# Merging the 32-block inverses of a gated DeltaNet with 128-row, half-width tiles padded by zeros

## The chip, the cores and the metric

The kernel runs on one core of one Trainium2 chip. The metric is the device time of one execution in microseconds (us). The five engines of the core are TensorE (PE in the profile, with its weight loads as PEld), VectorE (DVE), ScalarE (ACT), GpSimd (POOL) and SyncE (SP, which here issues the DMAs).

## The reference

One inference step of a two-layer decoder trunk for 512 prompt tokens and 8 x 8 sample tokens, with a width of 1024, all in float32. Layer 0 mixes by causal pooling, layer 1 by a gated DeltaNet; each mixer is followed by a SwiGLU block (inner width 2816), and all have RMS norms before and after. What the change touches is the triangular solve in the chunked delta rule:

```python
a_mat = jnp.where(strict, jnp.einsum('bhnid,bhnjd->bhnij', kb, k) * decay, 0.0)
t_mat = a_mat + jnp.eye(CHUNK, dtype=jnp.float32)
solve = functools.partial(lax.linalg.triangular_solve, left_side=True, lower=True, unit_diagonal=True)
u = solve(t_mat, v * beta[..., None])
w = solve(t_mat, kb * jnp.exp(gc)[..., None])
...
def step(S, inp):
    v_new = u_i - jnp.einsum('bhck,bhkv->bhcv', w_i, S)
    o_i = jnp.einsum('bhck,bhkv->bhcv', qd_i, S) + jnp.einsum('bhcs,bhsv->bhcv', qk_i, v_new)
    S = S * gl_i[..., None, None] + jnp.einsum('bhck,bhcv->bhkv', kd_i, v_new)
```

There are 16 value heads of 128 x 128. The kernel works in chunks of 128 tokens, four for the prompt.

## The kernel before, in words

The whole program is recorded first and then ordered by a planner (class Plan). Each operation is put with its engine or engines, an estimated cost and the operations that it must follow; a list scheduler with 40 rounds of search then writes an order for all engines. Two accesses to one PSUM tile, one of which writes, always keep the order in which they were recorded; accesses to SBUF tiles keep it only where their regions meet. Where the planner expects PE to stand free it puts in fillers, matmuls of ones on ones into a free PSUM bank (ps_w in the profile). Its costs know the height and the width of a matmul's tile.

The DeltaNet runs in four groups of four value heads. For a group, project computes queries, keys and values with matmuls (ps_m) and a short convolution on DVE. Then core does this:

- It forms Uw, a tile of 128 partitions x 16 matrices x 128 columns: for each of 4 heads and 4 chunks the transposed triangular matrix of the solve.
- inv32 inverts the four 32 x 32 blocks on the diagonal of each of the 16 matrices at once on DVE (tiles "ia" and "ii"), and ends with four DVE transposes, one for each row block of 32 partitions, from "ii" into the diagonal blocks of Uw. Beside it runs the preparation of the sample tokens (sample_front).
- The merge turns the inverses of 32-blocks into those of 64-blocks and then of 128. T01 holds diagonal blocks transposed back by DVE. For two lower blocks each: a product of an off-diagonal block of Uw with a block of T01 goes to PSUM and by ACT to Rs; a second product with a diagonal block goes by ACT, negated, into the off-diagonal block of Uw. The same is then done once more with 64-blocks, through R2. The matmuls use tiles of the array of 32 x 32 and then of 64 x 64, in places given by tile_position (row, column).
- scan goes through the four chunks with the merged Uw and carries the state S from chunk to chunk; sample_heads does the sample tokens with states loaded by DMA into the tiles tagged "ia" and "ii", and with km in the tile tagged "T01".

The matmuls of the next group's project (in the last group, of the output projection out0) are free to run beside all this. Uw is one tile for all groups, so the forming of Uw for the next group waits for the scan of this one.

Tiles of one tag share memory; with bufs=1 the next tile of the tag waits for the last reader of the one before. PSUM is handed out in rings of banks by bank(tag): "s" has three banks, "k" two.

In the profile all recorded operations have line 281, the line at which the planner issues them, so tiles are told apart by name; digits at the end of a name are dropped: T is T01, R is R2, Rs is Rs. An fp32 matmul leaves two records of a MATMUL and two of a LDWEIGHTS.

Of the kernel before, what the change touches and what calls it, by code (L numbers as in the profile page):

```python
# [11 lines left out]
F32 = mybir.dt.float32  # L12
F32R = mybir.dt.float32r
I32 = mybir.dt.int32
AF = mybir.ActivationFunctionType
# [5 lines left out]
P = 128  # L21
# [474 lines left out]
def hybrid_kernel(  # L496
# [11 lines left out]
    PE, ACT, DVE, POOL, SP = (plan.engine(**{name: real}) for name, real in (  # L508
        ("PE", nc.tensor), ("ACT", nc.scalar), ("DVE", nc.vector), ("POOL", nc.gpsimd), ("SP", nc.sync)))
# [76 lines left out]
    def bank(tag, shape=(P, 512)):  # L586
        i = RING[tag][turns[tag] % len(RING[tag])]
        turns[tag] += 1
        idle = psp.tile([P, 512], F32, name="ps_w", tag="b%d" % i, bufs=1)
        t = psp.tile(list(shape), F32, name="ps_" + tag, tag="b%d" % i, bufs=1)  # L590
        plan.bank(i, idle, t)
        return t
# [243 lines left out]
    with ExitStack() as s0:  # L836
        xp = pool("xp0", stack=s0)
        x = xp.tile([P, NC, T], F32, name="x")
        y = {o0: xp.tile([P, NC, n], F32, name="y%d" % o0) for o0, n in HALVES}
        tp = pool("tp0", stack=s0)  # L840
        with ExitStack() as st:
# [12 lines left out]
            for g0, src in ((G_MPRE, norm_mix_pre), (G_MPOST, norm_mix_post), (G_FPRE, norm_ffn_pre),  # L854
                            (G_FPOST, norm_ffn_post), (G_PS, pool_scale)):
                n = src.shape[0] * NC
# [72 lines left out]
            for hi, (o0, n) in enumerate(HALVES):  # L929
                tag = "AB"[hi]  # L930
# [77 lines left out]
    def inv32(ap_, W):  # L1008


        A = ap_.tile([P, 32, 32], F32, name="ia", tag="ia", bufs=1)
        XT = ap_.tile([P, 2, 512], F32, name="ii", tag="ii", bufs=1)
        X = XT[:, 0].rearrange("p (j i) -> p j i", j=32)
        for b in range(4):
            s = slice(32 * b, 32 * b + 32)
            DVE.transpose(A[s], W[s, :, 32 * b:32 * b + 32].rearrange("p h i -> p i h").unsqueeze(2)
                          .to_broadcast([32, 32, 2, 16]))
            yield 1.2
        EITHER.tensor_copy(X, eye2)
        for m in range(31, 0, -1):  # L1020
            lo = m // 2
            tv = XT[:, 1, :m * (16 - lo)].rearrange("p (j i) -> p j i", j=m)
            DVE.tensor_tensor(tv, A[:, m, :m].unsqueeze(2).to_broadcast([P, m, 16 - lo]),
                              X[:, m:m + 1, lo:].to_broadcast([P, m, 16 - lo]), op=mult)
            DVE.tensor_tensor(X[:, :m, lo:], X[:, :m, lo:], tv, op=sub)
            yield 2 * (m * (16 - lo) + 60) / 700
        for b in range(4):
            s = slice(32 * b, 32 * b + 32)
            DVE.transpose(W[s, :, 32 * b:32 * b + 32].rearrange("p h (i d) -> p i d h", d=2),
                          X[s].rearrange("p j i -> p i j"))  # L1030
            yield 0.6


    with ExitStack() as st:
# [214 lines left out]
        def braid(a, b, n):  # L1249

            for i, c in enumerate(a):
                yield c
                if i % n == n - 1:
                    c = next(b, None)
                    if c is not None:
                        yield c
            yield from b
# [208 lines left out]
        def core(G, pr_, out):  # L1466
            qk, vt, qks, vs, kt = pr_
            QD = cp_.tile([P, 4, SPANS, P], F32, name="QD", tag="QD", bufs=1)
            oss = cp_.tile([P, SP1, 4], F32, name="oss", tag="oss", bufs=2)
            POOL.memset(oss[:, SPANS], 1.0)  # L1470
            out.append(oss)
            TQ = cp_.tile([P, 2, 2, P], F32, name="TQ", tag="TQ", bufs=1)
            Ts, Qs = TQ[:SMP], TQ[SMP:, :, :, :SMP]
            ks = cp_.tile([P, 2, P], F32R, name="ks", tag="ks", bufs=1)
            Uv = Uw.rearrange("p (h s) i -> p h s i", h=4)
            h4 = slice(4 * G, 4 * G + 4)
            for s in range(SPANS):
                ps = bank("s", (P, 4, P))
                gts = cp_.tile([P, 2, 4, P], F32R, name="gts", tag=("T01", "ia")[s % 2], bufs=1)
                for i, src in enumerate((gH, gL)):  # L1480
                    gt = gts[:, i]
                    EITHER.tensor_tensor(gt, t_le.unsqueeze(1).to_broadcast([P, 4, P]),
                                      src[:, s, h4].bitcast(F32).unsqueeze(2).to_broadcast([P, 4, P]), op=mult)
                    PE.matmul(ps, t_gt_r, gt, start=i == 0, stop=i == 1)
                de = QD[:, :, s]
                ACT.activation(de, ps, AF.Exp)
                EITHER.tensor_tensor(de, de, t_le.unsqueeze(1).to_broadcast([P, 4, P]), op=mult)
            for s in range(SPANS):
                sl = slice(s * P, (s + 1) * P)
                de = QD[:, :, s]  # L1490
                for hd in range(2):
                    pk = bank("k")
                    pkv = pk[:, :2 * P].rearrange("p (x i) -> p x i", x=2)
                    PE.matmul(pkv, qk[:, hd, 0, sl], qk[:, hd, :, sl], start=True, stop=True)
                    for e in range(2):
                        h = 2 * hd + e
                        DVE.scalar_tensor_tensor(out=Uv[:, h, s], in0=pkv[:, 0],
                                                 scalar=bet[:, s, 4 * G + h:4 * G + h + 1], in1=de[:, h],
                                                 op0=mult, op1=mult)
                    DVE.tensor_tensor(QD[:, 2 * hd:2 * hd + 2, s], pkv[:, 1:2].to_broadcast([P, 2, P]),  # L1500
                                      de[:, 2 * hd:2 * hd + 2], op=mult)
                    yield 0.6
            yield from braid(inv32(cp_, Uw), sample_front(G, qks, Ts, Qs, ks), 8)
            T01 = cp_.tile([P, 16, 64], F32, name="T01", tag="T01", bufs=1)
            POOL.memset(T01[:32, :, 32:], 0.0)
            for b, o in ((0, 0), (1, 32), (2, 0)):
                q = slice(32 * b, 32 * b + 32)
                DVE.transpose(T01[q, :, o:o + 32], Uw[q, :, 32 * b:32 * b + 32])
                yield 0.6

            Rs = cp_.tile([P, 16, 32], F32, name="Rs", tag="Rs", bufs=1)
            Q = [slice(32 * b, 32 * b + 32) for b in range(4)]
            prs = [bank("k", (P, 16, 32)) for _ in range(2)]
            for u in range(16):
                for i, b0 in enumerate((0, 2)):
                    PE.matmul(prs[i][Q[b0 + 1], u], Uw[Q[b0], u, Q[b0 + 1]], T01[Q[b0], u, 0:32], start=True, stop=True,
                              tile_position=(32 * b0, 32 * b0 + 32))
            for i, b0 in enumerate((0, 2)):
                ACT.activation(Rs[Q[b0 + 1]], prs[i][Q[b0 + 1]], AF.Copy)
            pus = [bank("s", (P, 16, 32)) for _ in range(3)]  # L1520
            for u in range(16):
                for i, (q, c) in enumerate(((1, 0), (3, 2), (1, 1))):
                    l, r = (Uw[Q[q], u, Q[q]], Rs[Q[q], u]) if i == 2 else (Rs[Q[q], u], Uw[Q[q], u, Q[q]])
                    PE.matmul(pus[i][Q[c], u], l, r, start=True, stop=True, tile_position=(32 * q, 32 * c))
            for i, b0 in enumerate((0, 2)):
                ACT.activation(Uw[Q[b0], :, Q[b0 + 1]], pus[i][Q[b0]], AF.Copy, scale=-1.0)
            ACT.activation(T01[Q[1], :, 0:32], pus[2][Q[1]], AF.Copy, scale=-1.0)

            R2 = cp_.tile([P, 16, 64], F32, name="R2", tag="ia", bufs=1)
            E = [slice(0, 64), slice(64, P)]  # L1530
            prs = [bank("k", (P, 8, 64)) for _ in range(2)]
            for u in range(8):
                for i in range(2):
                    PE.matmul(prs[i][E[i], u], Uw[:64, 8 * i + u, 64:], T01[:64, 8 * i + u], start=True, stop=True,
                              tile_position=(0, 64 * i))
            for i in range(2):
                ACT.activation(R2[64:, 8 * i:8 * i + 8], prs[i][E[i]], AF.Copy)
            pus = [bank("s", (P, 8, 64)) for _ in range(2)]
            for u in range(8):
                for i in range(2):  # L1540
                    PE.matmul(pus[i][E[i], u], R2[64:, 8 * i + u], Uw[64:, 8 * i + u, 64:], start=True, stop=True,
                              tile_position=(64, 64 * i))
            for i in range(2):
                ACT.activation(Uw[:64, 8 * i:8 * i + 8, 64:], pus[i][E[i]], AF.Copy, scale=-1.0)
            yield from braid(scan(G, qk, vt, QD, kt, Uv, oss), sample_heads(G, qks, vs, Ts, Qs, ks, oss), 2)

        def gate_norm(pr_, oss):
# [238 lines left out]
```

## Time and profile before

| what | value |
|---|---|
| median of 3 runs | 1669.38 us (1666.42 to 1671.91) |
| profiled execution, time | 1672.26 us |
| profiled execution, span | 1670.6 us |
| mean granted clock of TensorE | 0.977 |
| PE busy | 1640.1 us, 98% |
| DVE busy | 1005.8 us, 60% |
| ACT busy | 696.3 us, 42% |
| POOL busy | 94.3 us, 6% |

The profile is of one execution; its times are in us from the start of its span. Busy time is the union of an engine's records; a matmul's record reaches beyond the start of the next one, since they are pipelined, so the distance between starts tells what one costs. The granted clock is the share of the full TensorE clock that the chip allowed.

### The profile page before, as it was taken

To read this page: it belongs to the slowest core of one execution; us is meant where nothing else is said; L and a number is where in the kernel's file an instruction comes from. 1 tells how busy PE (TensorE), PEld (TensorE's weight loads), DVE (VectorE), ACT (ScalarE), POOL (GpSimd) and SP (SyncE) were. 2 spreads that over 40 slices of the span, in tenths; PEclk is the share of its full clock that TensorE was granted. 3 is DMA by queue.
4 is the path that set the end of the run, shared out by engine and by line. 5 is a ranking of instruction groups with operands and counts; after the bars stand their busy time and mean duration, and the time that the engine had idled before them with its cause. 6 is when DMAs were issued, how large, how long until landed. Compare 5 with 4: busy or idle time off the path is not lost.

```text
span 1670.6 us, 30880 instructions
## 1 busy us (share of the span) xinstructions
PE 1640.1 (98%) x12495; PEld 1584.6 (95%) x12495; DVE 1005.8 (60%) x2096; ACT 696.3 (42%) x1423; POOL 94.3 (6%) x231
## 2 busy tenths in 40 slices
PE   9999999999999899999999999999999999999998
PEld 8999999999999789998999899899999999999997
DVE  6874223332597996797899689767596222223345
ACT  7653222222466534463453355324364223222244
POOL 4000000000010200010120011000000000000000
PEclk9999999999999998998999899899999999999999
DMA  6354322232356114334333422554755223323333
GB/s 173 103 154 124 92 86 78 75 102 75 114 166 164 51 52 134 87 97 119 97 97 94 135 70 78 159 168 145 237 146 150 85 77 90 93 70 89 89 109 112
DMA packets 329814, 185.27 MB, mean 111 GB/s; under 512 B 12236, under 2 KB 324141, under 8 KB 329408
## 3 DMA queue, kind: packets, MB, share of 16 engines
q1 hardware_dynamic: 329671, 183.30, 37.9%
q8 instruction: 98, 1.61, 0.4%
q14 instruction: 45, 0.36, 0.1%
HBM read 157.73 MB, written 25.77 MB: 110 GB/s over the span
## 4 chain that ended last, share of the span: by engine, by line
PE 86%; DVE 7%; ACT 3%; issue 2%; POOL 1%; DMA 1%; DVEq 0%; ACTq 0%; SPq 0%; POOLq 0%
PE ps_B L281 30%; PE ps_A L281 23%; PE ps_m L281 17%; PE ps_s L281 6%; PE ps_k L281 5%; PE ps_x L281 2%; DVE ii L281 2%; PE ps_e L281 1%; DVE wl L281 1%; PE ps_n L281 1%; ACT L281 1%; ACT wh L281 1%; PE ps_g L281 1%; DMA yo<-y_d 1%; DVE Uw L281 0%
## 5 line engine op out<-in xcount | busy, mean ns | idle before, releaser
L281 ACT ACTIVATE wh<-wraw 128x1024 fp32r<-128x1024 f32 (+1 forms) x259 | 267.7, 1036 | 493.3 <-PE ps_A L281 161.6
L281 DVE TENSOR_TENSOR wl<-wraw,wh 128x1024 fp32r<-128x1024 f32 (+1 forms) x252 | 304.7, 1213 | 275.1 <-PE ps_A L281 104.8
L281 PE MATMUL ps_m<-hH,wh 128*128 128x320 f32 (+1 forms) x832 | 245.9, 319 | 1.0 <-ACT u L281 0.6
L281 PE MATMUL ps_m<-hH,wl 128*128 128x320 f32 (+1 forms) x832 | 242.0, 314 | 4.7 <-DVE wl L281 4.7
L281 PE MATMUL ps_m<-hL,wh 128*128 128x320 f32 (+1 forms) x832 | 242.4, 314 | 1.2 <-DVE hL L281 1.2
L281 PE MATMUL ps_B<-hH,wl 128*128 128x320 f32 x768 | 219.3, 311 | 0.0
L281 PE MATMUL ps_B<-hH,wh 128*128 128x320 f32 x768 | 219.1, 311 | 0.0
L281 PE MATMUL ps_B<-hL,wh 128*128 128x320 f32 x768 | 218.0, 311 | 0.0
L281 PE MATMUL ps_A<-hH,wh 128*128 128x256 f32 x768 | 206.6, 283 | 2.2 <-DVE yo L281 1.8
L281 PE MATMUL ps_A<-hL,wh 128*128 128x256 f32 x768 | 206.2, 283 | 0.0
L281 PE MATMUL ps_A<-hH,wl 128*128 128x256 f32 x768 | 203.6, 283 | 0.0
L281 PEld LDWEIGHTS ps_m<-hH,wl 128*128 128x128 f32 x832 | 153.9, 192 | 9.0 <-DVE wl L281 4.9
L281 PEld LDWEIGHTS ps_m<-hH,wh 128*128 128x128 f32 x832 | 153.7, 193 | 7.5 <-ACT u L281 1.9
L281 PEld LDWEIGHTS ps_m<-hL,wh 128*128 128x128 f32 x832 | 154.2, 192 | 5.3 <-DVE hL L281 2.1
L281 PEld LDWEIGHTS ps_A<-hH,wh 128*128 128x128 f32 x768 | 141.9, 190 | 2.9 <-issue 2.5
L281 PEld LDWEIGHTS ps_A<-hL,wh 128*128 128x128 f32 x768 | 142.2, 190 | 0.2
L281 PEld LDWEIGHTS ps_A<-hH,wl 128*128 128x128 f32 x768 | 141.4, 190 | 0.1
L281 PEld LDWEIGHTS ps_B<-hH,wl 128*128 128x128 f32 x768 | 139.5, 189 | 0.6 <-DVE wl L281 0.5
L281 PEld LDWEIGHTS ps_B<-hH,wh 128*128 128x128 f32 x768 | 139.5, 189 | 0.2
L281 PEld LDWEIGHTS ps_B<-hL,wh 128*128 128x128 f32 x768 | 139.2, 189 | 0.1
L281 PE MATMUL ps_B<-aH,wl 128*128 128x320 f32 x352 | 102.8, 311 | 0.0
L281 PE MATMUL ps_B<-aH,wh 128*128 128x320 f32 x352 | 102.5, 311 | 0.0
(386 smaller groups left out, 3119.5 us busy)
## 6 DMA issues: line engine op xcount, KB each, us to landing
wraw<-in_ffn_w_in_dram SPq DMA_DIRECT2D x112, 512.0 KB
wraw<-in_gdn_w_in_dram SPq DMA_DIRECT2D x56, 512.0 KB
wraw<-in_ffn_w_out_dram SPq DMA_DIRECT2D x48, 448.0 KB
wraw<-in_gdn_w_out_dram SPq DMA_DIRECT2D x24, 512.0 KB
wraw<-in_ffn_w_out_dram SPq DMA_DIRECT2D x16, 512.0 KB
St<-in_state_gdn_rec_dram SPq DMA_DIRECT2D x32, 256.0 KB
out_dram<-St SPq DMA_DIRECT2D x32, 256.0 KB
z_d<-zz SPq DMA_DIRECT2D x16, 288.0 KB
```

What stands on the lines that cost most here:

```text
L281: calls[e](*a, **k)
```

## The change

The steps of the merge keep their products, but each matmul now takes 128 rows of the array and 64 of its columns, with operands padded by zeros, two matmuls for the left and the right half of the columns in turn. T01, Rs2 (in the slot "ii") and the lower half of R2 (in "ia") are set to zero by POOL first. T01 holds the transposed block 0 in its first 32 columns and block 2 in the others for the first step; after it, block 1 is transposed into the second columns and block 2 set back to zero. The second step is two series, pt with 32 and pu with 64 streamed columns, and its results leave PSUM in six copies of 256 columns instead of three of 512. Rs, formerly a tile of its own that shared a tag with a scratch tile, is dropped for Rs2.

```diff
+            T01 = cp_.tile([P, 16, 64], F32, name="T01", tag="T01", bufs=1)
+            Rs = cp_.tile([P, 16, 64], F32, name="Rs2", tag="ii", bufs=1)
+            R2 = cp_.tile([P, 16, 64], F32, name="R2", tag="ia", bufs=1)
+            for t in (T01, Rs, R2[:64]):
+                POOL.memset(t, 0.0)
+            def odd(un):
+                return Uw[:, un].rearrange("p (x b) -> p x b", x=2)[:, :, 32:]
+            def products(pr, l, r, n=64):
+                for u in range(8):
+                    for i in range(2):
+                        PE.matmul(pr[E[i], u, :n], l(8 * i + u), r(8 * i + u), start=True, stop=True,
+                                  tile_position=(0, 64 * i))
+            def out_of(pr, to, j, c, scale=1.0):
+                for i in range(2):
+                    q = 64 * i + 32 * j
+                    ACT.activation(to(slice(8 * i, 8 * i + 8)), pr[q:q + 32, :, c], AF.Copy, scale=scale)
-            for b, o in ((0, 0), (1, 32), (2, 0)):
-                q = slice(32 * b, 32 * b + 32)
-                DVE.transpose(T01[q, :, o:o + 32], Uw[q, :, 32 * b:32 * b + 32])
+            lo, up = slice(0, 32), slice(32, 64)
+            for b, c in ((0, lo), (2, up)):
+                DVE.transpose(T01[Q[b], :, c], Uw[Q[b], :, Q[b]])
-            prs = [bank("k", (P, 16, 32)) for _ in range(2)]
+            pr = bank("k", (P, 16, 32))
             for u in range(16):
-                for i, b0 in enumerate((0, 2)):
-                    PE.matmul(prs[i][Q[b0 + 1], u], Uw[Q[b0], u, Q[b0 + 1]], T01[Q[b0], u, 0:32], start=True, stop=True,
-                              tile_position=(32 * b0, 32 * b0 + 32))
+                for i, c in enumerate((lo, up)):
+                    PE.matmul(pr[E[i], u], Uw[:, u, E[i]], T01[:, u, c], start=True, stop=True, tile_position=(0, 64 * i))
...
+            ACT.activation(Rs[Q[1], :, lo], pr[Q[1]], AF.Copy)
+            ACT.activation(Rs[Q[3], :, up], pr[Q[3]], AF.Copy)
+            DVE.transpose(T01[Q[1], :, up], Uw[Q[1], :, Q[1]])
+            POOL.memset(T01[Q[2], :, up], 0.0)
-            pus = [bank("s", (P, 16, 32)) for _ in range(3)]
-            for u in range(16):
-                for i, (q, c) in enumerate(((1, 0), (3, 2), (1, 1))):
-                    l, r = (Uw[Q[q], u, Q[q]], Rs[Q[q], u]) if i == 2 else (Rs[Q[q], u], Uw[Q[q], u, Q[q]])
-                    PE.matmul(pus[i][Q[c], u], l, r, start=True, stop=True, tile_position=(32 * q, 32 * c))
+            pu, pt = bank("s", (P, 8, 64)), bank("s", (P, 8, 64))
+            products(pt, lambda un: Uw[:, un, :64], lambda un: Rs[:, un, lo], 32)
+            products(pu, lambda un: Rs[:, un], odd)
+            out_of(pt, lambda us: T01[Q[1], us, lo], 1, lo, -1.0)
+            out_of(pu, lambda us: Uw[Q[0], us, Q[1]], 0, lo, -1.0)
+            out_of(pu, lambda us: Uw[Q[2], us, Q[3]], 1, up, -1.0)
...
+            pr = bank("k", (P, 8, 64))
+            products(pr, lambda un: Uw[:, un, 64:], lambda un: T01[:, un])
             for i in range(2):
-                ACT.activation(R2[64:, 8 * i:8 * i + 8], prs[i][E[i]], AF.Copy)
+                ACT.activation(R2[64:, 8 * i:8 * i + 8], pr[E[i]], AF.Copy)
+            pu = bank("s", (P, 8, 64))
+            products(pu, lambda un: R2[:, un], lambda un: Uw[:, un, 64:])
             for i in range(2):
-                ACT.activation(Uw[:64, 8 * i:8 * i + 8, 64:], pus[i][E[i]], AF.Copy, scale=-1.0)
+                ACT.activation(Uw[:64, 8 * i:8 * i + 8, 64:], pu[E[i]], AF.Copy, scale=-1.0)
```

More of the change, by code (lines that the diff above doesn't have):

```diff
@@ L1503, in core @@
             yield from braid(inv32(cp_, Uw), sample_front(G, qks, Ts, Qs, ks), 8)
+            Q = [slice(32 * b, 32 * b + 32) for b in range(4)]
+            E = [slice(0, 64), slice(64, P)]
             T01 = cp_.tile([P, 16, 64], F32, name="T01", tag="T01", bufs=1)
-            POOL.memset(T01[:32, :, 32:], 0.0)
-            for b, o in ((0, 0), (1, 32), (2, 0)):
-                q = slice(32 * b, 32 * b + 32)
-                DVE.transpose(T01[q, :, o:o + 32], Uw[q, :, 32 * b:32 * b + 32])
+            Rs = cp_.tile([P, 16, 64], F32, name="Rs2", tag="ii", bufs=1)
@@ L1509, in core @@
+            def out_of(pr, to, j, c, scale=1.0):
[5 more added lines that the diff above has]
+                DVE.transpose(T01[Q[b], :, c], Uw[Q[b], :, Q[b]])
                 yield 0.6
-            Rs = cp_.tile([P, 16, 32], F32, name="Rs", tag="Rs", bufs=1)
-            Q = [slice(32 * b, 32 * b + 32) for b in range(4)]
@@ L1513, in core @@
-            prs = [bank("k", (P, 16, 32)) for _ in range(2)]
+            pr = bank("k", (P, 16, 32))
             for u in range(16):
-                for i, b0 in enumerate((0, 2)):
-                    PE.matmul(prs[i][Q[b0 + 1], u], Uw[Q[b0], u, Q[b0 + 1]], T01[Q[b0], u, 0:32], start=True, stop=True,
-                              tile_position=(32 * b0, 32 * b0 + 32))
-            for i, b0 in enumerate((0, 2)):
-                ACT.activation(Rs[Q[b0 + 1]], prs[i][Q[b0 + 1]], AF.Copy)
-            pus = [bank("s", (P, 16, 32)) for _ in range(3)]
@@ L1521, in core @@
-            for u in range(16):
-                for i, (q, c) in enumerate(((1, 0), (3, 2), (1, 1))):
-                    l, r = (Uw[Q[q], u, Q[q]], Rs[Q[q], u]) if i == 2 else (Rs[Q[q], u], Uw[Q[q], u, Q[q]])
-                    PE.matmul(pus[i][Q[c], u], l, r, start=True, stop=True, tile_position=(32 * q, 32 * c))
-            for i, b0 in enumerate((0, 2)):
-                ACT.activation(Uw[Q[b0], :, Q[b0 + 1]], pus[i][Q[b0]], AF.Copy, scale=-1.0)
-            ACT.activation(T01[Q[1], :, 0:32], pus[2][Q[1]], AF.Copy, scale=-1.0)
@@ L1529, in core @@
[L1529 to L1535, printed above, removed]
-            for i in range(2):
-                ACT.activation(R2[64:, 8 * i:8 * i + 8], prs[i][E[i]], AF.Copy)
@@ L1538, in core @@
[L1538 to L1542, printed above, removed]
+                for i, c in enumerate((lo, up)):
+                    PE.matmul(pr[E[i], u], Uw[:, u, E[i]], T01[:, u, c], start=True, stop=True, tile_position=(0, 64 * i))
+            ACT.activation(Rs[Q[1], :, lo], pr[Q[1]], AF.Copy)
```

## The prediction

> **What bounds the kernel now.** I read the page first, then the busy time by stretch, then TensorE's rows in order of time, and last the rows of DVE, ACT and POOL around the merges.
>
> ```profile
> PE 1640.1 (98%) x12495; PEld 1584.6 (95%) x12495; DVE 1005.8 (60%) x2096; ACT 696.3 (42%) x1423; POOL 94.3 (6%) x231
> ...
> PE 86%; DVE 7%; ACT 3%; issue 2%; POOL 1%; DMA 1%; DVEq 0%; ACTq 0%; SPq 0%; POOLq 0%
> ```
>
> TensorE (PE) is busy 98% and carries 86% of the chain that ended last. I cut four stretches, each from the first merge matmul of a group to the moment the clock is back:
>
> ```profile
> 621.87:638.26 16.39, 16.39 (x251) 14.81 (x250) 7.50 (x10) 5.64 (x11) 0.00 (x0) 0.58 0.36 101
> 775.40:791.86 16.46, 16.46 (x250) 14.89 (x250) 8.87 (x12) 5.58 (x11) 0.00 (x0) 0.59 0.50 146
> 918.25:935.22 16.97, 16.17 (x252) 14.41 (x252) 9.50 (x13) 5.64 (x12) 0.00 (x0) 0.60 0.61 172
> 1064.83:1081.99 17.16, 17.00 (x248) 15.42 (x249) 8.22 (x13) 7.27 (x15) 0.14 (x1) 0.60 0.38 111
> ```
>
> The columns are length, busy time of PE, weight loads, DVE, ACT and POOL, granted clock, DMA share and GB/s. Four times about 16.7 us, 67 us in all, run at a mean clock of 0.58 to 0.60, though PE is never free for more than 0.8 us. The second of the four, nearer, with two other stretches for comparison:
>
> ```profile
> 774.79:778.20 3.41, 3.41 (x93) 3.07 (x92) 3.32 (x4) 2.17 (x4) 0.00 (x0) 1.00 0.00 0
> 778.20:791.86 13.66, 13.66 (x167) 12.20 (x165) 6.13 (x10) 4.01 (x7) 0.00 (x0) 0.50 0.60 176
> 638.26:641.67 3.41, 3.41 (x19) 3.02 (x17) 1.29 (x2) 0.00 (x0) 0.04 (x1) 1.00 0.00 0
> 976.18:983.00 6.82, 6.82 (x26) 6.08 (x26) 5.34 (x12) 3.31 (x12) 0.59 (x3) 0.50 0.00 0
> ```
>
> The clock is full in the 3.41 us in which the merges start, then exactly half for 13.66 us, which is four times 3.41. Elsewhere it fell for 6.82 us, twice 3.41. So the clock is decided in windows of 3.41 us. In the first of these rows PE was busy all of the time, so busy time is not what is counted. What PE did there:
>
> ```profile
> 775.40 2.15 PE L281 MATMUL ps_k<-T,Uw 32*32 32x32 f32 x64
> 777.45 1.15 PE L281 MATMUL ps_s<-Rs,Uw 32*32 32x32 f32 x27
> ...
> 780.12 1.97 PE L281 MATMUL ps_k<-T,Uw 64*64 64x64 f32 x30
> 782.02 0.66 PE L281 MATMUL ps_s<-Uw,Rs 32*32 32x32 f32 x12
> 782.60 0.47 PE L281 MATMUL ps_k<-T,Uw 64*64 64x64 f32 x2
> 783.00 1.11 PE L281 MATMUL ps_x<-ident,vt 128*128 128x128 f32 x4
> 784.05 2.39 PE L281 MATMUL ps_s<-Uw,R 64*64 64x64 f32 x32
> ```
>
> The columns are start, length, operands (array rows*columns used) and count. From 775.40 on the tiles are 32*32, one sixteenth of the array. How long columns stream at full clock, other rows show:
>
> ```profile
> 585.53 0.45 PE L281 MATMUL ps_k<-qks 128*64 128x128 f32 x4
> 585.80 0.40 PE L281 MATMUL ps_k<-ident,qks 128*64 128x128 f32 x4
> 586.12 0.39 PE L281 MATMUL ps_m<-hH,wl 128*128 128x256 f32 x1
> ```
>
> The second four records of 128 columns, run two by two, take about 0.22 us before the next changeover: 0.11 us for 128 columns, so 0.053 for 64 and 0.027 for 32. Streamed time weighted by area gives the window at 774.79 at most 0.61 us of full-array work and 88 x 0.027/16 = 0.15 us of tiles, 0.76 of 3.41 or 0.22, and the clock fell. The way back bounds the limit: from 785.03 to 788.44 stand 1.4 us of the last row, 19 records of a quarter array (19 x 0.053/4 = 0.25), and 2.0 us of full-array work at half clock (1.0): at most 0.37, and the clock stayed down; the next window, all full-array at half clock, gives at most 0.50, and it came back. I take this measure, with a limit between 0.22 and 0.50, likely near 0.37. Zeros seem to count as work:
>
> ```profile
> 633.46 2.07 PE L281 MATMUL ps_s<-vt,Uw 128*128 128x128 f32 x8
> ...
> 637.64 3.92 PE L281 MATMUL ps_k<-St,kx 128*128 128x256 f32 x16
> ```
>
> kx is 128 columns wide with 16 that aren't zero, and 638.26 to 641.67 holds little but its matmuls; the clock stayed full (third row of the stretches above).
>
> [...] By busy time alone PE was already full, padding could not help, and the result is rival D below; the trace disagrees, since the clock fell after 3.41 us without a gap.
>
> **The change, part by part.** In the trace's names T is T01 and R is R2; one fp32 matmul leaves two records.
>
> Matmuls. Before, a group has 64 + 96 + 32 + 32 = 224 records: 2.05 us (775.40 to 777.45), then 2.67 to 780.12, 2.88 to 783.00 and 2.39 for the last step, 10.0 us in all. The rest of that stretch, 16.46 - 10.0 = 6.5 us, is scan, projection and transposes, nearly all at half clock; at full clock I put it at half, 3.3 us. After, there are 32 + 16 + 16 + 16 + 16 = 96 matmuls of 128 rows by 64 columns, 192 records. The rows at 585.53 have that shape: eight records in 0.59 us, changeovers included. Two column halves do run side by side. For 32 or 64 streamed columns the weight load should set the pace:
>
> ```profile
> L281 PEld LDWEIGHTS ps_k<-T,Uw 32*32 32x32 f32 x256 | 7.8, 107 | 1.9 <-DVE T L281 1.6 <-issue 0.2
> ...
> L281 PEld LDWEIGHTS ps_k<-ident,qks 128*64 128x64 f32 x32 | 2.4, 136 | 0.7 <-issue 0.7
> ```
>
> The mean load of 32 columns takes 107 ns, of 64 columns 135 or so: near 30 ns for 32 columns. One 32-column tile in single file took 2.05 us / 64 = 32 ns a record, so I estimate 32 + 28 = 60 ns for a 64-column tile: 192 x 60 / 2 = 5.8 us side by side, 11.5 us in single file. I take 5.8: the steps write both halves into one PSUM tile, the planner orders all accesses to one PSUM tile as written, and they are written in turn. A stretch becomes 5.8 + 3.3 = 9.1 us, 7.6 less than the mean of 16.7.
>
> [...]
>
> Clock. By area the new tiles fill the array in pairs. Of the 60 ns, 32 columns stream for 27, so the 1.9 us of the first step and the 0.95 us of the first half of the second count about 0.45, the 64-column steps about 0.9. With projection matmuls in the gaps a window has 0.5 to 0.8, over the limit; a window of both light steps around an empty gap would have (1.9 + 0.95) x 0.45 / 3.41 = 0.38, just at it if the limit is 0.37. I charge one lost window, 1.7 us, to one group in five.
>
> The start. Before, the first step reads 32 rows of one block, and DVE's order shows it:
>
> ```profile
> 618.65 2.32 DVE L281 STREAM_TRANSPOSE Uw<-ii 32x512 f32<-32x512 f32 x2
> 621.01 1.44 DVE L281 STREAM_TRANSPOSE T<-Uw 32x512 f32<-32x512 f32 x2
> 622.47 2.14 DVE L281 STREAM_TRANSPOSE Uw<-ii 32x512 f32<-32x512 f32 x2
> ```
>
> It began at 621.87, when the first T was done. The new first step reads all rows of Uw and T01 and alternates its halves, so it waits for all four Uw transposes and two T transposes: 2.32 + 2.14 + 1.44 = 5.9 us instead of 3.1, 2.8 us later. In three groups projection matmuls cover that; in the last one there are few:
>
> ```profile
> 1061.64 2.17 PE L277 MATMUL ps_w<-ones 128*128 128x128 f32 x18
> 1064.83 1.92 PE L281 MATMUL ps_k<-T,Uw 32*32 32x32 f32 x58 [1.01 <-DVE T L281]
> ```
>
> 18 filler matmuls on ones and 1.0 us idle stood there before, so in that group the two moved transposes, 2.2 us, cost in full. The third T transpose and a second memset of T01 come behind the first step, beside the second: hidden, 0.7 us (1.44 / 2) and half the memset below if not.
>
> ACT, POOL, SP and PSUM:
>
> ```profile
> L281 ACT ACTIVATE T<-ps_s 32x512 f32<-32x512 f32 x4 | 2.4, 588 | 3.1 <-PE ps_s L281 3.1
> ```
>
> ```profile
> L281 POOL MEMSET kx<- 128x1088 f32 x1 | 1.0, 1012 | 0.0
> ```
>
> ACT has six copies of 256 instead of three of 512 columns; one of 256 costs between half of 0.59 us and all of it, I take 0.40: 6 x 0.40 - 3 x 0.59 = 0.6 us more. PE waits there for up to four of them (1.6 us), covered by projection matmuls, on the chain if they are gone. POOL gets three memsets of 1024 columns, near the 1.0 us of 1088, and one of 512, instead of one of 512: 3 us more. T01 and R2 are free early; Rs2 takes the slot "ii" after the last transpose out of it and is needed only after the first step, 1.4 + 1.9 us later: nothing, 1.0 us if POOL is late. The state load into "ii" used to start right after those transposes, now after the second step, nearer to the other load that its reader needs anyway; it waits in SP's queue, with weight loads behind it. Nothing, up to 1 to 2 us if the queue stands. Fewer PSUM banks are held: nothing.
>
> The order of the whole program is planned anew. A clock drop like that at 976.18 may come or go: plus or minus 3.4 us, taken as zero.
>
> **The sum.** If PE alone sets the time: 4 x 7.6 = 30.4, less 2.2 and less 1.4 for a lost window, 27 us. But the groups also form a chain through Uw. From the end of the inverses to the first scan matmul it takes 633.46 - 618.65 = 14.8 us now; after: 5.9 + 1.9 + 1.2 (two copies) + 1.9 + 0.8 + 0.95 + 1.2 + 0.95 + 1.2 = 16.0, 0.9 for six hand-overs of 0.14 (621.01 + 0.72 to 621.87), less 0.6 of overlap, 16.3: 1.5 longer. The scan's start then runs at full clock, 638.26 - 633.46 = 4.8 us halved, 2.4 gained. If the chain alone sets the time: 4 x 0.9 = 4 us. Which one?
>
> ```profile
> 622.00:775.40 153.40, 152.17 (x1221) 143.41 (x1220) 126.69 (x296) 74.21 (x173) 10.78 (x31) 0.96 0.36 103
> 775.40:918.25 142.85, 141.55 (x1139) 132.31 (x1138) 124.17 (x295) 65.64 (x166) 18.20 (x35) 0.95 0.36 103
> ```
>
> From merge to merge PE is busy 99%, for the first end; DVE is busy 83 to 87%, for the second. I take the middle, 15.5 us: 1672.26 - 15.5 = 1656.8 for a profiled run, which was 2.9 us above the median of the runs, so 1654.
>
> **The rivals.**
> A, the forecast: clock held, gain shared between PE and chain; 1654, its own range 1646 to 1664. Chance 0.55.
> B, PE sets all: 1669.4 - 27 = 1642. For it: PE's 99%. Against: DVE's 83 to 87%, and the longer chain. Chance 0.15.
> C, the clock is held but the chain sets the end, or the halves run in single file (11.5 + 3.3 = 14.8 us a stretch, 1.9 saved): 1669.4 - 4 to - 8, taken as 1665. For it: the 18 fillers ahead of the last merges show that the chain sets parts already. Against: PE's 99% in the other groups. Chance 0.20.
> D, slower: the clock falls all the same, because padding zeros in the streamed operand or short matmuls don't count. A 64-column record in a pair costs 63 ns at half clock (1.90 us / 30, 64*64), so PE's merges take 1.9 + 128 x 0.063 = 10.0 us, as before, and the later start, 2.8 us in each group, is not paid back: 1669.4 + 11 = 1680. It decides if the clock after the first step reads 0.50 for 13.66 us again. Against: kx. Chance 0.10.
>
> **How the numbers follow.** No change means within 0.3%, 5 us, about what a measurement of this kernel can tell. Nearly all of A and B and a little of C are faster, 0.72; the rest of C and D's milder cases are the same, 0.18; slower is 0.10. The range leaves out D and the lower half of B: 1642 to 1672.
>
> **What would show it.** In the profile after: granted clock 1.00 through the merges; records of 128*64 tiles in pairs, 64 of the first step in about 1.9 us; the first step behind six transposes; fillers on ones or idle time ahead of it if the chain sets the end. The prediction is wrong if the clock still reads 0.50 for 13.66 us there, if the first step takes nearer 3.8 us, or if the saved PE time comes back as fillers in the scan.

## The result and the profile after

The changed kernel took 1659.3 us (median of 5 runs, 1653.4 to 1661.3) against 1671.9 us for the kernel before on the same chip: a ratio of 0.9925, 95% interval 0.9897 to 0.9953, 12.6 us faster. The forecast was 1654, the range 1642 to 1672. The profiled execution took 1661.3 us with a span of 1659.6; the one before had 1672.3 and 1670.6. Among the five runs the time follows the granted clock, from 1653.4 us at 0.994 to 1661.3 at 0.988, and that clock differs from one execution to the next; every profile and stage table below is of one execution, and the one of the changed kernel is its slowest.

From the page of the changed kernel, the engines' busy time and the chain that ended last:

```profile
PE 1631.1 (98%) x12415; PEld 1576.5 (95%) x12415; DVE 1001.5 (60%) x2095; ACT 700.5 (42%) x1436; POOL 105.9 (6%) x244
...
PE 84%; DVE 8%; ACT 3%; DMA 2%; issue 1%; SPq 0%; POOL 0%; DVEq 0%; ACTq 0%
```

TensorE is as full as before (98%), with 9 us less to do, and the chain is still mostly its own. The totals don't show what happened; the stretches do. Here are the four groups from the first merge matmul to the first matmul of the scan, and then two windows of the clock (3.41 us) in the second group (columns: length, busy time of PE, weight loads, DVE, ACT, POOL, granted clock, DMA share, GB/s):

```profile
627.97:642.03 14.06, 14.06 (x238) 12.69 (x238) 9.80 (x12) 8.94 (x18) 1.81 (x5) 1.00 0.31 95
775.61:788.81 13.20, 13.20 (x234) 11.92 (x235) 6.37 (x7) 7.20 (x15) 0.74 (x2) 1.00 0.53 154
910.60:924.90 14.30, 14.30 (x242) 12.94 (x242) 6.39 (x10) 6.86 (x14) 1.47 (x2) 1.00 0.58 167
1050.72:1067.10 16.38, 16.38 (x225) 14.98 (x225) 5.86 (x10) 7.20 (x16) 0.74 (x2) 0.69 0.24 69
```

```profile
774.50:777.91 3.41, 2.50 (x56) 2.13 (x54) 3.31 (x5) 0.57 (x2) 0.95 (x1) 1.00 0.01 2
777.91:781.32 3.41, 3.41 (x87) 3.24 (x85) 0.99 (x2) 1.18 (x2) 0.52 (x1) 1.00 0.84 230
```

In three groups of four the clock stays full through the merges; in the last it falls. Note the first window: PE was idle for 0.9 of its 3.41 us and the clock held (1.00 in the next row), where before PE had no gap at all (busy 3.41 of 3.41 us from 774.79 on) and it fell (0.50).

The matmuls of the merges in the second group, TensorE's rows in order of time (start, length, operands, rows*columns of the array, count, idle time before and what ended it):

```profile
775.61 0.30 PE L281 MATMUL ps_k<-T,Uw 128*64 128x32 f32 x2 [0.91 <-DVE T L281]
775.84 0.41 PE L281 MATMUL ps_m<-hH,wl 128*128 128x320 f32 x1
...
776.53 2.05 PE L281 MATMUL ps_k<-T,Uw 128*64 128x32 f32 x62
778.51 0.39 PE L281 MATMUL ps_m<-hH,wh 128*128 128x256 f32 x1
...
779.62 1.06 PE L281 MATMUL ps_s<-Rs,Uw 128*64 128x32 f32 x29
...
780.57 1.07 PE L281 MATMUL ps_s<-Uw,Rs 128*64 128x64 f32 x30
...
781.66 0.39 PE L281 MATMUL ps_m<-hL,wh 128*128 128x256 f32 x1
...
782.80 0.33 PE L281 MATMUL ps_k<-T,Uw 128*64 128x64 f32 x2
783.06 0.39 PE L281 MATMUL ps_m<-hH,wh 128*128 128x256 f32 x1
...
783.73 1.15 PE L281 MATMUL ps_k<-T,Uw 128*64 128x64 f32 x30
784.81 0.39 PE L281 MATMUL ps_m<-hL,wh 128*128 128x256 f32 x1
...
786.79 1.15 PE L281 MATMUL ps_s<-Uw,R 128*64 128x64 f32 x30
```

The reader should see two things. The 62 records of the first step start 30 ns apart (1.83 us from the first start to the last), where the prediction's estimate for single file was 60: the two column halves do run side by side. And the first and the third step (the fourth too, at 785.89) begin with two records alone, after which projection matmuls (ps_m) run until the other half follows: the halves alternate, so the step waits for both.

The span can be cut at four kinds of events in each group: the first transpose of the inverses back into Uw, the first scan matmul (vt,Uw), the last output matmul of the scan (vn,QD), and the next group's first transpose. What follows the last group's scan is the tail. From the starts of those rows, in us, sums over the groups, with the time of half clock between 600 and 1150 us:

| kernel | start to first inverses | merges (4) | scans (4) | scan to next inverses (3) | tail | span | half clock |
|---|---|---|---|---|---|---|---|
| before | 618.7 | 61.9 | 265.9 | 197.7 | 526.5 | 1670.6 | 61.4 |
| changed | 623.7 | 78.1 | 232.2 | 195.9 | 529.7 | 1659.6 | 10.2 |

The merges themselves, as a stage, became 16 us **longer**. The scans became 34 us shorter, and that is the whole gain. Merges and scans together are 17.5 us shorter: 9.4, 7.8 and 2.4 in the first three groups, while the last one is 2.1 longer. The span gained only 11.0 of them, since the start and the tail, where the edit changes nothing, took 5.0 and 3.2 us more. (From scan to next inverses it was 1.8 less.) What connects merges and scans is the work beside them. The projection matmuls alone (rows of ps_m; busy time and count of PE first), in merges and scan of the first two groups, before and then after:

```profile
618.65:633.46 14.81, 4.93 (x28) 4.00 (x26) 0.87 (x3) 0.70 0.29 80
633.46:708.60 75.14, 57.68 (x292) 44.05 (x292) 4.38 (x13) 0.97 0.38 109
772.30:787.73 15.43, 4.49 (x28) 3.89 (x26) 0.36 (x1) 0.69 0.47 137
787.73:851.20 63.47, 37.32 (x191) 28.28 (x191) 2.96 (x9) 0.97 0.39 109
```

```profile
623.70:642.03 18.33, 11.62 (x72) 9.60 (x70) 0.82 (x2) 1.00 0.34 103
642.03:704.30 62.27, 43.94 (x214) 32.23 (x213) 3.74 (x11) 1.00 0.42 118
770.20:788.81 18.61, 10.60 (x64) 8.64 (x63) 1.19 (x3) 1.00 0.55 157
788.81:841.40 52.59, 24.51 (x128) 18.47 (x127) 2.08 (x7) 1.00 0.41 114
```

Before, 28 projection records fitted into the merges of each of these groups and 292 and 191 stood in the scans; after, 72 and 64 fit into the merges, and 214 and 128 are left. At full clock the merges have room for the projections, and the scan is rid of them. No fillers stand in the scans, before or after, so the time that PE saved did not come back as such. In the same two scans the second step's first matmul (rs,Uw) came 25.4 and 17.6 us after the first (vt,Uw) before, and 11.7 and 5.8 after. What stood in between in the second group, before and after (nearly all of the St,kx products have moved behind rs,Uw there; in the other three groups as many still stand in between as before):

```profile
787.73 2.08 PE L281 MATMUL ps_s<-vt,Uw 128*128 128x128 f32 x8
...
791.74 3.68 PE L281 MATMUL ps_k<-St,kx 128*128 128x256 f32 x16
...
800.39 0.59 PE L281 MATMUL ps_k<-S,qk 128*128 128x256 f32 x2
...
805.37 0.38 PE L281 MATMUL ps_s<-rs,Uw 128*128 128x128 f32 x2
```

```profile
788.81 0.60 PE L281 MATMUL ps_s<-vt,Uw 128*128 128x128 f32 x4
...
792.01 1.03 PE L281 MATMUL ps_k<-S,qk 128*128 128x256 f32 x4
...
794.61 0.60 PE L281 MATMUL ps_s<-rs,Uw 128*128 128x128 f32 x4
```

### The profile page after: what moved, and what is told of

Its sections match the earlier page's. It is cut to its first block, busy times and chain, and to the rows that moved or that the text cites. A ratio compares the mean times of both kernels' runs of the same rounds, so it can differ in the third digit from the quotient of the medians.

```text
span 1659.6 us, 30728 instructions
## 1 busy us (share of the span) xinstructions
PE 1631.1 (98%) x12415; PEld 1576.5 (95%) x12415; DVE 1001.5 (60%) x2095; ACT 700.5 (42%) x1436; POOL 105.9 (6%) x244
## 4 chain that ended last, share of the span: by engine, by line
PE 84%; DVE 8%; ACT 3%; DMA 2%; issue 1%; SPq 0%; POOL 0%; DVEq 0%; ACTq 0%
PE ps_B L281 29%; PE ps_A L281 24%; PE ps_m L281 16%; PE ps_k L281 5%; PE ps_s L281 5%; PE ps_x L281 2%; PE ps_e L281 1%; DVE ii L281 1%; DVE wl L281 1%; PE ps_n L281 1%; ACT L281 1%; DVE Uw L281 1%; ACT wh L281 1%; DMA yo<-y_d 0%; DVE ia L281 0%
## 5 line engine op out<-in xcount | busy, mean ns | idle before, releaser
L281 ACT ACTIVATE wh<-wraw 128x1024 fp32r<-128x1024 f32 (+2 forms) x259 | 266.8, 1035 | 506.2 <-PE ps_B L281 204.0
L281 DVE TENSOR_TENSOR wl<-wraw,wh 128x1024 fp32r<-128x1024 f32 (+2 forms) x252 | 299.6, 1195 | 299.2 <-PE ps_A L281 72.3
L281 PE MATMUL ps_B<-hH,wl 128*128 128x320 f32 x768 | 222.5, 311 | 1.1 <-DVE wl L281 1.1
L281 PE MATMUL ps_B<-hL,wh 128*128 128x320 f32 x768 | 222.7, 311 | 0.1
L281 PE MATMUL ps_B<-aL,wh 128*128 128x320 f32 x352 | 103.8, 311 | 0.0
```

The lines of the kernel that those rows point to most:

```text
L281: calls[e](*a, **k)
```

## The experiments

The comparisons are with the kernel before, run on the same chip; differences of a few us between two of these kernels are judged after the runs on order, below.

**Is it the padding, or the fewer and steadier matmuls?** The same tiles and counts, with the rows that hold nothing left out of all products but one:

```
-PE.matmul(pr[E[i], u], Uw[:, u, E[i]], T01[:, u, c], ..., tile_position=(0, 64 * i))
+PE.matmul(pr[E[i], u], Uw[Q[2*i], u, E[i]], T01[Q[2*i], u, c], ..., tile_position=(64 * i, 64 * i))
-products(pt, lambda un: Uw[:, un, :64], lambda un: Rs[:, un, lo], 32)
+products(pt, lambda un: Uw[Q[1], un, :64], lambda un: Rs[Q[1], un, lo], 32, 32)
 (and 64 rows in the last two steps)
```

> The changed kernel with its 64-column tiles, side by side in pairs, but with only the rows that hold anything: 32 rows in the first step and in the T01 product, 64 in the last two steps; the product of Rs with the odd blocks stays at 128. Same number of matmuls (192 records a group), same copies, same result. Theory 1, area: a record of the first step counts a quarter of what it did, the last two steps half, so with 0.45 of the time streaming they come to 0.11 and 0.45 of the array; the clock goes to 0.50 in the merges of most groups, for 10 to 14 us each, and most of the gain is lost: 1664 to 1674 us. Theory 2, fewer and steadier matmuls: padding is beside the point, the time stays at that of the change, 1656 to 1662 us; the first step may even start sooner, since it no longer reads all blocks.

Measured: 1681.5 us, ratio 1.0069 (1.0041 to 1.0097), slower even than before. The four groups, from the first merge matmul to the scan, and the first step of the third group:

```profile
624.54:640.64 16.10, 15.14 (x212) 13.29 (x213) 10.08 (x16) 8.69 (x19) 1.47 (x2) 0.66 0.13 36
775.10:790.62 15.52, 15.18 (x215) 13.03 (x215) 6.41 (x10) 5.44 (x12) 1.47 (x2) 0.66 0.50 138
924.14:935.30 11.16, 10.51 (x214) 9.20 (x213) 5.84 (x7) 6.47 (x14) 1.47 (x2) 1.00 0.43 122
1062.40:1080.40 18.00, 16.59 (x209) 14.04 (x210) 7.16 (x10) 6.60 (x15) 1.47 (x2) 0.62 0.18 53
```

```profile
924.14 2.05 PE L281 MATMUL ps_k<-T,Uw 32*64 32x32 f32 x64
```

The clock falls in three groups (13.66, 13.66 and 17.07 us), as theory 1 expects, and the time is 8 us beyond the upper end of what it gave. In the third group it happened to hold, and there the 32-row step takes 2.05 us, no longer and no shorter than with 128 rows: padding cost no streaming time here and saved none. What it brought is the clock, 1.00 in the merges of three groups instead of one. Theory 2 has fallen. The stages say the same without the scatter of the total that other orders bring (below): merges and scans together take 332.6 us here, as much as before the change (323.7 to 332.6 with three seeds) and more than after it (305.0 to 315.3). The projection records that begin in the four merges are 34, 43, 44 and 17 here, 70, 63, 76 and 26 with the padding, and 26, 25, 28 and 4 before. Streamed time weighted by area, worked out from the shapes and starts of the records, was 0.24 to 0.31 in the windows after which the clock fell, 0.34 to 0.39 in the third group's, after which it stayed.

**Does the first step need all rows?** Only the first of those two edits:

> The changed kernel with the first step alone on 32 rows (64 columns stay); the other steps keep their 128 rows. Its first half then needs one block of Uw and one transpose, as before the change. Theory 1a, the wait for all six transposes is what costs in the groups with little other work, and lets the clock fall in the last group: the first step starts 2 to 3 us sooner, the drop in the last group goes, 1652 to 1657 us. Theory 1b, by area the first step now counts a quarter (0.11 of the array while it runs) and the clock falls in more groups than one: 1662 to 1670 us. If neither matters: 1657 to 1662 us.

Measured: 1665.8 us (1661.3 to 1673.1, 12 runs), ratio 0.9971 (0.9955 to 0.9988). In the first three groups the first step started 3.1 to 3.7 us after the inverses instead of 4.3 to 5.4, and the clock held there too (windows no lower than 0.37, thanks to the projections in the gaps), so 1b is wrong. In the last group the drop was 13.66 us instead of 10.24, so 1a is wrong as well:

```profile
1049.96 0.38 PE L281 MATMUL ps_m<-hL,wh 128*128 128x256 f32 x1 [1.95 <-POOL hL L281]
...
1051.45 0.41 PE L281 MATMUL ps_k<-T,Uw 32*64 32x32 f32 x2 [0.52 <-DVE T L281]
```

There PE ran out of fillers and waited 1.95 us for an operand of the projection. Of the 5.5 us by which its span is longer than the changed kernel's, 4.2 lie in the tail (533.9 against 529.7 us), where the code is the same, and merges and scans together are as long (310.9 against 310.3); the time by itself proves nothing for or against the edit.

**Can extra work hold the clock in the old kernel?** The kernel before with 22 products of ones and the identity strewn over each group's steps:

```
+def extra(to):
+    PE.matmul(to.rearrange("p a b -> p (a b)"), ones, ident, start=True, stop=True)
 for u in range(16):
+    if u % 2 == 0 and u < 14:
+        extra(prs[0][:, u:u + 4])
     ...
```

> The kernel before the change, its merges on 32 and 64 row tiles as they were, with 22 extra 128x128x128 products of ones and the identity in each group's four steps, written where the steps write afterwards (4 x 22 x 0.22 = 19 us of TensorE work that computes nothing). Theory 1, area: with them each window of the merges counts over 0.40, the clock stays full there, and the 27 us that the half clock cost are had back against the 19 us: 1658 to 1672 us, no slower than before. Theory 2, the gain of the change came from fewer matmuls and the clock falls as before: the extra work costs 19 us at full clock and up to 38 at half: 1690 to 1710 us.

Measured: 1736.5 us, ratio 1.0388 (1.0366 to 1.0411): a miss for theory 1, and beyond theory 2's range too. Rows of the second group, and its windows:

```profile
782.45 0.31 PE L281 MATMUL ps_k<-T,Uw 32*32 32x32 f32 x4
782.69 0.49 PE L281 MATMUL ps_k<-ident,ones 128*128 128x128 f32 x2
783.11 0.31 PE L281 MATMUL ps_k<-T,Uw 32*32 32x32 f32 x4
```

```profile
781.11:784.52 3.41, 3.41 (x33) 2.57 (x32) 3.29 (x5) 1.09 (x4) 0.33 (x2) 1.00 0.50 141
784.52:787.94 3.42, 3.42 (x86) 2.92 (x86) 0.72 (x1) 1.18 (x2) 0.00 (x0) 1.00 0.90 233
787.94:811.83 23.89, 23.89 (x178) 19.45 (x173) 2.27 (x3) 4.12 (x7) 0.00 (x0) 0.50 0.14 40
```

What I had wrong was the price. A product and the way back to the small tiles takes 0.42 us (782.69 to 783.11), not 0.22. Its two records stream for 0.11 us each (fillers of the same shape start 0.11 us apart in the changed kernel, 36 of them in 4.18 us at 1044.15), so the 0.22 was the streaming alone: switching between 128-row and 32-row tiles took the other 0.20 us, about as much again as the product. So the extra work made the stretch longer, not denser: by area the window at 781.11 counts 0.42 (the clock stayed), the one at 784.52 counts 0.19 (it fell), the next six 0.14 to 0.27 (it stayed down) and the last one 0.39, after which it came back. The area rule holds in each of these windows; the kernel just did not reach the limit. In the changed kernel, where both kinds of tiles have 128 rows, the switch was cheaper: the two records at 775.61, which stream 32 columns, and the way back to the projections take 0.23 us.

**How much is the order?** The program's order comes from a random search in the planner. Both kernels with two other seeds (`SEED = 1`, `2`):

> The changed kernel with another seed for the random search of the planner that orders the whole program; the same instructions in another order. If the order is a matter of a few us, as the prediction took it (plus or minus 3.4 us): 1655 to 1664 us, and the clock drops stand at other places. If the gain of the change were an accident of the new order, it could come to 1665 or more.

> The kernel before the change with another seed for the random search of the planner that orders the program. The changed kernel with this seed came to 0.9970 of the kernel before, against 0.9925 with its own. If the replanned order is worth some 4 us either way, this comes to 1665 to 1678 us, with the four drops of 13.66 us in its merges as they were. If the seeds of the changed kernel differ for a reason of the change (orders that starve TensorE in the merges), this one stays within 2 us of 1671.

> The same with a third seed: 1665 to 1678 us if orders are worth 4 us either way, within 2 us of 1671 if they are worth little without the change.

> The changed kernel with a third seed. If the change is worth 27 us of TensorE time that the chain gives half of back, whatever the order: 1655 to 1667 us, no drops in the merges of the first three groups, one in the last. If 1659 was a lucky order: 1667 us or more.

| seed | before: us, ratio | changed: us, ratio | changed over before |
|---|---|---|---|
| 0 | 1671.9, 1 | 1659.3, 0.9925 (0.9897 to 0.9953) | 0.9925 |
| 1 | 1688.2, 1.0090 (1.0067 to 1.0113) | 1666.8, 0.9970 (0.9947 to 0.9992) | 0.988 |
| 2 | 1662.3, 0.9946 (0.9928 to 0.9965) | 1660.3, 0.9922 (0.9899 to 0.9945) | 0.998 |

The order alone moves the kernel before over 26 us, far more than the 4 us expected, and the changed one over 7.5; with seed 1 both kernels, and with seed 2 the kernel before, lie outside the ranges given for orders worth 4 us. The change is faster by 0.8 and 1.2% with two seeds; the 0.2% with the third is not clear of the noise, since its two intervals overlap. The average is 12 us. The scans tell the same without that scatter: 265.9, 259.6 and 262.8 us before, 232.2, 234.5 and 229.3 after, and half clock 61.4, 58.0 and 47.8 us against 10.2, 17.1 and none. Merges and scans together are 17.5, 17.3 and 18.7 us shorter, though the last group gains nothing with any seed (2.1 longer, 0.1 shorter, 0.7 longer). The changed kernel reaches its first inverses 5.0, 6.6 and 5.6 us later, and its profiles show more half clock ahead of them (20.5 against 6.8 us, 23.9 against 13.7, 13.7 against 3.4); whether that comes with the change or by chance is not shown.

**What is a us of TensorE worth, and a us of the chain?** Three products of the low-order correction fewer (or three more, overwritten) in each half projection of all groups but the first (G = 1 to 3 in the code); and the copies of R2 out of PSUM made seven times:

```
-PE.matmul(ps, wh[:, k], al, start=False, stop=False)
+if k >= less:                                   # 3 where G is 1 to 3
+    PE.matmul(ps, wh[:, k], al, start=False, stop=False)
```

```
+for _ in range(3 if G else 0):                  # the kernel with more
+    PE.matmul(ps, w[0][:, 0], h_of(hi)(0)[0], start=True, stop=True)
 mm3(ps, w, h_of(hi), NC)
```

> The changed kernel with 3 of the 24 products of every half projection of groups 1 to 3 left out (part of the low-order correction of the projections, so its output is a little off): 80 halves x 3 x 0.134 us = 32 us less of TensorE work beside the merges and scans, the chain of inverses, merges and scans as it is. If TensorE alone sets the time there: 1659 - 32 = 1627 us. If the chain takes over at once: 1655 to 1660. The prediction's middle, half and half: 1643. The order is planned anew, which the seeds put at up to 8 us either way.

> The changed kernel with 3 more products in each of the same 80 halves, overwritten by the first real one: 32 us more of TensorE work at the same places. If TensorE sets the time after the change too: 1691 us; if the chain has taken over and TensorE has slack: 1660 to 1670.

```
+for _ in range(7):
     ACT.activation(R2[64:, 8 * i:8 * i + 8], pr[E[i]], AF.Copy)
```

> The changed kernel with each of the two copies of R2 out of PSUM in the merges made 7 times: 12 more copies of 0.4 to 0.6 us one behind the other, 5 to 7 us more in the chain of each group, 20 to 28 us in all, and no TensorE work. If the chain of inverses, merges and scans sets the time: 1680 to 1687 us. If it is covered by TensorE's other work in three groups and shows only in the last one: 1662 to 1668 us.

| kernel | median, ratio to before | start | merges | scans | to next inverses | tail | span |
|---|---|---|---|---|---|---|---|
| changed | 1659.3, 0.9925 (0.9897 to 0.9953) | 623.7 | 78.1 | 232.2 | 195.9 | 529.7 | 1659.6 |
| 32 us of PE less | 1651.0, 0.9874 (0.9849 to 0.9899) | 622.6 | 78.6 | 222.5 | 199.3 | 527.7 | 1650.8 |
| 32 us of PE more | 1678.1, 1.0041 (1.0027 to 1.0055) | 618.8 | 84.3 | 255.3 | 188.0 | 528.3 | 1674.7 |
| 28 us of chain more | 1679.8, 1.0043 (1.0026 to 1.0059) | 625.4 | 107.4 | 217.6 | 200.8 | 529.3 | 1680.5 |
| rows only | 1681.5, 1.0069 (1.0041 to 1.0097) | 621.4 | 76.2 | 256.4 | 192.6 | 530.1 | 1676.8 |

32 us less of TensorE brought 8 us, a quarter, which is no more than another seed can bring; 32 us more cost 19, six tenths; the longer chain cost 20, just under what a chain that sets the time had been given: its 29 us stand in the merges, and the scans gave 15 back. So neither limit sets the time alone, as far as one order of each kernel can tell, and it is the scan in which TensorE's load is felt: with more load its length goes from 232 to 255 us, with less to 222. From scan to next inverses it is 188 to 201 us whatever is done to TensorE.

**The drop in the last group.** In the changed kernel's last merge, its rows and two windows:

```profile
1044.15 4.18 PE L277 MATMUL ps_w<-ones 128*128 128x128 f32 x36
1050.72 0.30 PE L281 MATMUL ps_k<-T,Uw 128*64 128x32 f32 x2 [2.39 <-DVE T L281]
...
1051.68 3.62 PE L281 MATMUL ps_k<-T,Uw 128*64 128x32 f32 x62
```

```profile
1047.56:1050.98 3.42, 1.03 (x10) 0.80 (x9) 3.29 (x5) 1.53 (x4) 0.95 (x1) 1.00 0.69 228
1050.98:1061.22 10.24, 10.24 (x138) 9.61 (x138) 4.38 (x9) 3.15 (x8) 0.52 (x1) 0.50 0.09 27
```

The fillers ended at 1048.3, DVE was still transposing, PE idled 2.39 us, and the window counted 0.20. Two kernels put products there that start when the inverses are done, 24 and then 12 of them:

```
 for m in range(31, 0, -1): ...
+if extra:                                       # 24, then 12, in the last group
+    pd = bank("k")
+    for _ in range(extra):
+        PE.matmul(pd[:, :P], ones, XT[:, 0, :P], start=True, stop=True)
```

> The changed kernel with 24 more products of 128x128x128 (ones by the result of the inverses, never read) in the last group alone, set to run when the inverses are done, while DVE transposes for 5.9 us. In that group fillers placed by the planner's clock ended 2.4 us before the first step could start, and the clock fell for 10.24 us. Theory 1, the drop there comes from TensorE starving ahead of the first step: the drop goes, the merges of the last group take 3 to 5 us less, 1654 to 1657 us. Theory 2, the first step is too light by area whatever stands ahead of it: the drop stays, the 24 products cost up to 5 us: 1659 to 1664 us.

> The changed kernel with 12 instead of 24 products on the result of the inverses in the last group. With 24 the drop in the last merge was gone, but the first step started at 1053.4 instead of 1050.7 us, behind them. With 12 (2.6 us) it starts at 1050 to 1051 and the clock should hold: 2 to 3 us less than with 24, 1654 to 1658 us. If the order planned anew decides: anything from 1655 to 1667.

With 24: 1658.9 us, 0.9922 (0.9897 to 0.9946). The drop is gone, but the first step stands behind the extra work, and the last merge is 21.1 us long instead of 21.6. With 12: 1651.9 us, 0.9898 (0.9871 to 0.9924):

```profile
1042.17 2.94 PE L281 MATMUL ps_k<-ii,ones 128*128 128x128 f32 x24 [0.42 <-DVE ii L281]
...
1047.85 0.30 PE L281 MATMUL ps_k<-T,Uw 128*64 128x32 f32 x2 [0.33 <-DVE sn L281]
...
1048.72 2.05 PE L281 MATMUL ps_k<-T,Uw 128*64 128x32 f32 x62
```

The first step runs at full clock in 2.05 us instead of 3.62, and the merge takes 19.3 us. That shows 2.3 us of the 7.4 by which its median is below the changed kernel's; the rest is spread over the other stages and no more than what another seed brings. It is the fastest kernel here that computes all of the reference, but by less than the order's scatter. Theory 1 fits the drop: it is gone in both kernels, while it stands in the last merge of six of the seven others that pad (not with seed 2), each seen in one execution. Its 3 to 5 us were too many.

## Why the prediction was right, and where not

The total was right and so was the clock as its cause; the parts of the sum were not, and the gain came in another stage than the sum had it.

- **Clock by area: right.** The granted clock is 1.00 in the merges of three groups, and rival D is out. The limit "between 0.22 and 0.50, likely near 0.37" stands: over all these kernels, between 600 and 1150 us, every window under 0.27 was followed by half clock and every one over 0.40 by full, while those between went either way (some records are missing in a trace, so the sums are a little rough). Of these 2270 windows, 120 of them followed by half clock, 6 to 10 stand on the wrong side of the best single limit, near 0.36 (how many depends on where in its record the streaming is put); weighted by used rows alone or columns alone it is about 20, by time alone about 80. So rows and columns both count in these runs, though how exactly they weigh is not settled: ahead of that stretch, in the kernel before with seed 1, a window from 527.7 to 531.1 us holds hardly more than products that use 32 of the 128 columns without a tile_position (ps_g), 0.20 by used area, and the clock stayed full. The kernel's own planner weighs a matmul by the same measure (work in class Plan), which the prediction doesn't say. Busy time alone does not tell the windows apart: the kernel with rows only had PE busy 15.2 of 15.5 us in the second group and fell to half (granted clock 0.66 over that stretch).
- **Matmuls: right in kind, 20% short.** Side by side, not single file: the records start 30 ns apart as forecast, 32 where 64 columns stream. The merges of the second group take 6.9 us of PE (0.23 + 1.98 for the first step, 2.04 for the second, and 0.26 + 1.08 for the third, from the starts of the rows, and as much for the fourth) instead of 5.8, since the four steps run in seven pieces, each of which pays a changeover of 0.1 to 0.2 us that the sum didn't have (the piece of two records at 775.61 takes 0.23 us, 0.06 at 30 ns a record).
- **The start: right, a little short.** The first step began 4.3 to 5.4 us after the first transpose of the inverses, against 3.0 to 3.2 before, but with two records alone; the others, which need all six transposes, followed after 6.2 to 7.3 us, where the sum had 5.9. The 18 fillers that stood ahead of the last merges are 18 records, so nine matmuls. In the last group the wait was 2.39 us, and the window was lost there in two seeds of three, for 10.24 us at half clock, 5.1 us of work, where I had charged 1.7 for a lost window: three fell instead of one.
- **The chain: the term "1.5 longer" was mis-sized.** It came out 3.5, 3.2, 2.9 and 6.7 us longer. Between the second step and the third the sum had two copies, 0.8 us. Six stand there, of which the two halves of the third step need four, and the planned order put projection matmuls ahead of its second half, which came at 783.73, after the fifth copy:

```profile
781.75 0.37 ACT L281 ACTIVATE Uw<-ps_s 32x256 f32<-32x256 f32 x1 [1.87 <-PE ps_s L281]
782.15 0.78 ACT L281 ACTIVATE T<-ps_s 32x256 f32<-32x256 f32 x2
782.96 1.16 ACT L281 ACTIVATE Uw<-ps_s 32x256 f32<-32x256 f32 x3
```

 From 781.75 to 783.73 are 2.0 us where the sum had 0.8. At the fourth step the second half came 0.9 us after the first (785.89 and 786.79), behind the second copy of R2 and more projections. The last group adds 3 us for its half clock.
- **"The middle": right by its size, not by its picture.** I added a gain in PE and a loss in the chain and took half. In truth the merges lost 16 us, and the scans gained 34, of which I had put 2.4 per group. A scan is a chain of small steps, and the planner's order puts projections between them (292 and 191 records of ps_m in the first two scans before, 214 and 128 after); a projection that the merges take in no longer stands in the scan. The kernels with TensorE's load changed point to the scan as the place where the load counts. That the moved state load did it, which also changes what stands between the first two scan steps, is unlikely: the kernel with rows only has the same move and scans of 256 us, and in three groups the St,kx products still stand between these steps, which all the same came closer (25.4 to 11.7, 16.2 to 10.9 and 26.0 to 22.9 us). It was not tried by itself.
- **"Replanned order, plus or minus 3.4 us": wrong.** It is 13 us either way for the kernel before. The forecast was on the mark to 5 us partly by luck; with seed 2 the change would have been no more than 2 us.
- **ACT, POOL:** POOL has 11.6 us more on the page, 2.9 per group as said, and nothing in the merges waits for it (the memsets of Rs2 end 1.2 to 4.5 us before the first copy into it); ACT has 4.2 us more instead of 2.4.

## What to carry to other kernels

In these runs the clock fell to half with TensorE fully busy, and what told those windows of 3.41 us from the others was streamed time times the used share of the array (between 600 and 1150 us every one under 0.27 was followed by half clock, every one over 0.40 by full). Rows cost nothing in streaming (a record every 29 ns with 32 rows, every 30 with 128) and counted for the clock, also where they held zeros. Where another trace shows the same drop, count that, and try to fill the array, with zeros if need be. Look for the gain in the stage that is freed of the backlog, not in the one that is changed. And where a planner or a seed decides the order, time the change under several seeds before believing 1%.

## What the hardware showed that was not expected

A full-array product between 32-row tiles (782.69 in the kernel with 22 extra products) took 0.42 us with the way back, 0.22 of it streaming; two records of a 128-row, 64-column tile between projections (775.61 in the changed kernel) took 0.23 us with the way back. A window with PE idle for 27% of it (774.50 in the changed kernel) kept the full clock, while windows with PE busy throughout (774.79 before) lost it.
